# One piece of weights moved behind four pairs in every twelve-step chunk of a hybrid encoder layer

## The chip, the core and the metric

The kernel runs on one core of one Trainium2 chip. The metric is device time in microseconds (us), the median of repeated executions. The engines are named as in the profile: PE does matrix products (PEld loads its stationary operand), DVE works elementwise on tensors, ACT applies functions and copies, POOL is not used here beyond the start, SP issues the transfers (DMAs). Every engine takes its own instructions in order; one that must wait holds up all behind it on the same engine.

## What is computed

An input of 256 tokens by 4096 features is normalised, multiplied by an input projection 4096 x 13312, cut into the operands of a gated short convolution and of a windowed attention with 16 heads, multiplied by an output projection 4096 x 4096, added to the stream and normalised again. All in float32.

```python
h = layer_norm(x, emb_ln_g, emb_ln_b)
p = h @ w_in                       # 256 x 13312
y_conv = c_b * centred_short_conv(c_c * c_h, conv_w) * silu(c_z)
y_attn = banded_window_attention(a_q, a_k, a_v, sink) * silu(a_z)
y = concatenate([y_conv, y_attn]) @ w_out
out = layer_norm(DN_ALPHA * h + y, ln_g, ln_b)
```

## The kernel before

**Products in two parts.** PE gets float32 accuracy from a cheaper type by splitting each operand into a high part (a copy rounded by ACT, tile `whi`, line 226) and the rest (a subtraction on DVE, tile `wlo`, line 230). Three products are kept: high by high, low input by high weights, high input by low weights. Within a step PE first runs all products with `whi` and then those with `wlo`.

**Chunks.** The 13312 columns of the input projection are 26 chunks of 512 columns, numbered 0 to 25: K, V, then for each of four head groups the gate z and the queries q (chunks 2 to 9), then for each of four channel groups four convolution operands (10 to 25). The order of work inside a chunk is a string in `ORDERS`, written by hand:

- `s` is a **piece**: 4 blocks of 128 rows of weights, 1 MB, 48 matmuls of 256 columns (`mm`, line 275).
- `S` is a **pair**: 2 blocks of 128 rows, 512 KB, multiplied by a scheme after Strassen with seven products instead of eight, that is 21 matmuls (`mm_pair`, lines 300 to 303). It needs sums of weight blocks (DVE, `sums`, lines 192 to 194, made for two neighbouring pairs at once when they are "coupled") and sums of blocks of x (`x_sums`, made once and used by all later chunks).

A chunk of twelve steps (chunks 3 to 25) has four pieces and eight pairs. Positions count from 0 to 11 in a chunk; S4 means the pair at position 4, s5 the piece at position 5.

**What a step issues.** The loop at lines 835 to 859 goes over all steps j and writes, in this order: the products of step j; ACT's high part for step j+3; whatever `later` holds for step j; the end of a chunk at its position 3 of the following chunk (`chunk_end`, `whole`, line 717); `loads(j)`; the weight sums of step j+4; DVE's low part for step j+3. There are three `whi` and three `wlo` buffers, so the high part of step j+3 waits until PE has finished the `whi` products of step j, and the low part until PE has finished step j.

**Loads.** `loads` hands weights to four slots of `wall` and, for pieces, to `w6` as well (from chunk 13 on also `w7` and `w8`). Coupled pairs have to lie in `wall`. The next load goes out at step j when the last user of its buffer is step j+2 or earlier, and it waits for that user's low part. All these loads go through SP in order.

**Attention between the steps.** The work of a head group is cut into tasks with fixed distances t from the first step of the chunk after its queries (`SPREAD`, lines 661 to 663; t = 0 is position 0 of that chunk). The last two heads end in the chunk that follows 24 steps later: with t = 24 the turned probabilities of the third head (`p_tr`), with t = 27 their low part on DVE (`p_lo`, line 641, tile `kp`), with t = 28 the product with V on PE (`pv`, lines 648 and 650) and the turned probabilities of the fourth head, t = 29 `out_z` on DVE (line 654), t = 30 `p_lo` and t = 31 `pv` of the fourth head, which are positions 3, 4, 5, 6 and 7 of chunks 6, 8, 10 and 12. I call these four chunks the **tail chunks**. A `pv` waits on PE for its `p_lo` on DVE, and all later products wait behind it.

Of the kernel before, what the change touches and what calls it, by code (L numbers as in the profile page):

```python
# [34 lines left out]
NPC = KT // PK  # L35
# [7 lines left out]
NP = 8  # L43
NP1 = 4
PAIRS = [0, 0, NP1] + [NP] * (len(IN_ORDER) - 3)
ORDERS = {0: "s" * 8, NP1: "sssSSsSsSs", NP: "sSSsSSSSsSSs"}
OUT = 100
OP = 4
OUT_ORDERS = ["s" * 8] * 2 + ["sSsSsSsSss"] * 5 + ["", ""]
# [6 lines left out]
def units(ci):  # L56


    q, p, us = -(-2 * PAIRS[ci] // PK), 0, []
    for u in ORDERS[PAIRS[ci]]:  # L60
        if u == "s":
# [40 lines left out]
def encoder_kernel(ctx: ExitStack, tc: tile.TileContext, x, emb_g, emb_b, wi, ws, conv_w, sink, wo, ln_g, ln_b, out):  # L102
# [397 lines left out]
    def build_tab():  # L500
        ti = pa.tile([P, 2, S], F32, name="ti", tag="s")
        nc.gpsimd.iota(ti, pattern=[[-P, 2], [1, S]], base=0, channel_multiplier=-1,
                       allow_small_or_imprecise_dtypes=True)
        tf = pa.tile([P, 2, S], F32, name="tf", tag="p", bufs=2)
        nc.vector.tensor_scalar(tf, ti, -1.0, None, op0=ALU.mult)
        nc.vector.tensor_tensor(tf, tf, ti, op=ALU.max)
        nc.vector.tensor_scalar(ti, tf, float(WINDOW), NEG, op0=ALU.is_gt, op1=ALU.mult)
        nc.vector.tensor_tensor(tab, ti, tf, op=ALU.subtract)
# [162 lines left out]
    def x_sums(p, t):  # L671

        x = xT[:, 2 * p:2 * p + 2, :]
        xf = t[:, 0:2 * S].rearrange("p (k t) -> p k t", k=2)
        nc.vector.tensor_tensor(xf, x[:, :, 0:S].bitcast(F32), x[:, :, S:2 * S].bitcast(F32), op=ALU.add)
        a11, a12, a21, a22 = (xf[:, k, i * HT:(i + 1) * HT] for i in range(2) for k in range(2))
        s = t[:, 2 * S:4 * S].rearrange("p (k t) -> p k t", k=4)
        for k, o0, o1, op in ((0, a21, a22, ALU.subtract), (3, s[:, 0, :], a11, ALU.subtract),
                              (1, a11, a21, ALU.subtract), (2, a12, s[:, 3, :], ALU.add)):
            nc.vector.tensor_tensor(s[:, k, :], o0, o1, op=op)  # L680
        if SC[p].shape[2] == 4:
            return halves(SC[p][:, 0, :, :], SC[p][:, 1, :, :], s)
        halves(SC[p][:, 0, :, :], SC[p][:, 1, :, :], s[:, 0:3, :])
        halves(x[:, 0, HT:2 * HT], x[:, 0, 3 * HT:4 * HT], s[:, 3, :])
# [97 lines left out]
        for hi, lo, y in y_parts(q):  # L782
            nc.vector.tensor_tensor(lo, y, hi.bitcast(F32), op=ALU.subtract)

    X_SUMS = [NPC + 2 + k for k in range(NP1)] + [2 * NPC + k for k in (1, 4, 6, 8)]
    build_tab()
    later = {}

    def at(j, fn, *a):
        later.setdefault(j, []).append((fn, a))  # L790
# [36 lines left out]
    nxt = n_pro + 7  # L827
    last0 = N_IN - len(ORDERS[PAIRS[-1]])
    for t, f, q in ((3, y_load, 0), (5, y_hi, 0), (6, y_lo, 0), (6, y_load, 1), (7, y_hi, 1), (8, y_lo, 1), (8, y_load, 2),
# [5 lines left out]
    for j in range(n_pro, N_IN):  # L835
# [9 lines left out]
        if kind == "pair" and q == PAIRS[ci] - 1:  # L845
            pair_copy(ci)
            at(j + 1, pair_sums, ci)
        if j in X_SUMS:
            x_sums(X_SUMS.index(j), pa.tile([P, 4 * S], F32, name="xs", tag="zT", bufs=2))
        if steps[j + 1][1] != ci or j == N_IN - 1:  # L850
# [318 lines left out]
```

## Time and profile before

| | |
|---|---|
| median of three runs | 1501.05 us (1500.09 to 1501.15) |
| the profiled execution: its own time | 1500.92 us |
| its span, first to last instruction | 1499.2 us |
| granted PE clock | 0.999 |
| ACT busy | 803.3 us (54%) |
| SP's queue q1, share of the 16 DMA engines | 57.3% |

The profile lists instructions with their start and duration in us. Matmuls overlap: a row shows one as 0.28 us, but in an unbroken run the next starts 0.11 us later. So a stretch without a wait is read from starts to starts, and a wait on PE is a start that comes later than the one before it by more than 0.11 us. Rows of two DVE instructions in a row overlap by some 0.07 us as well, and are read in the same way. "[0.58 <-DVE kp L641]" behind a row is the idle time before it, and what ended it.

### The profile page before, as it was taken

How to read it: one execution, taken by the hardware profiler on the slowest of the kernel's cores; microseconds unless marked ns; L12 is line 12 of the kernel's file. 1: busy time of each engine (PE TensorE's matmuls, PEld its weight loads, DVE VectorE, ACT ScalarE, POOL GpSimd, SP SyncE). 2: the span in 40 equal slices, each digit the busy share in tenths (PEclk: the TensorE clock that was granted, in tenths of full speed). 3: DMA queues.
4: the chain of work that ended last, by engine and by line, in shares of the span. 5: the costliest groups of instructions: out<-in, count | busy, mean ns of one | idle time of the engine just before them, and what ended most of it. 6: DMA issues, size and time to landing. Idle time of an engine off the chain costs nothing.

```text
span 1499.2 us, 29810 instructions
## 1 busy us (share of the span) xinstructions
PE 1482.4 (99%) x12878; PEld 1465.4 (98%) x12878; DVE 1338.4 (89%) x1384; ACT 803.3 (54%) x687; POOL 1.3 (0%) x7
## 2 busy tenths in 40 slices
PE   7999999999999999999999999999999999999998
PEld 4999999999999999999999999999999999999997
DVE  7768999898999999999999999999998688888876
ACT  5544656766666665655555555555555444444431
POOL 0000000000000000000000000000000000000000
PEclk9999999999999999999999999999999999999999
DMA  8545465555554556646545655556558656756663
GB/s 318 217 183 196 164 217 189 192 197 208 180 204 176 190 201 209 230 177 224 200 182 219 231 198 197 225 204 241 191 207 313 233 201 220 290 215 230 219 237 113
DMA packets 71365, 316.17 MB, mean 211 GB/s; under 512 B 8545, under 2 KB 12609, under 8 KB 50113
## 3 DMA queue, kind: packets, MB, share of 16 engines
q1 hardware_dynamic: 70224, 312.43, 57.3%
q8 instruction: 101, 1.65, 0.4%
q10 hardware_dynamic: 1008, 1.84, 0.3%
q14 instruction: 32, 0.25, 0.0%
HBM read 305.23 MB, written 8.91 MB: 210 GB/s over the span
## 4 chain that ended last, share of the span: by engine, by line
PE 93%; DVE 3%; ACT 1%; issue 1%; DMA 1%; SPq 0%; ACTq 0%; DVEq 0%
PE acc L275 39%; PE acc L957 20%; PE pacc L301 6%; PE pacc L300 6%; PE pacc L303 6%; PE acc L301 4%; PE acc L300 4%; PE acc L303 4%; DVE wlo L230 1%; PE att L518 1%; ACT whi L226 1%; DVE st L354 0%; PE acc L404 0%; DMA wall<-in_ws 0%; DVE wall L192 0%
## 5 line engine op out<-in xcount | busy, mean ns | idle before, releaser
L226 ACT ACTIVATE whi<-wall 128x1792 fp32r<-128x1792 f32 (+1 forms) x284 | 501.7, 1772 | 464.6 <-DVE wall L194 149.7
L230 DVE TENSOR_TENSOR wlo<-wall,whi 128x1792 fp32r<-128x1792 f32 (+1 forms) x284 | 593.4, 2096 | 75.9 <-ACT whi L226 64.3
L275 PE MATMUL acc<-whi,xT 128*128 128x256 f32 x3584 | 427.6, 276 | 0.0
L275 PEld LDWEIGHTS acc<-whi,xT 128*128 128x128 f32 x3584 | 415.8, 188 | 0.0
L275 PE MATMUL acc<-wlo,xT 128*128 128x256 f32 x1792 | 221.3, 275 | 0.0
L275 PEld LDWEIGHTS acc<-wlo,xT 128*128 128x128 f32 x1792 | 211.4, 188 | 0.0
L226 ACT ACTIVATE whi<-w 128x2048 fp32r<-128x2048 f32 x73 | 140.7, 1927 | 114.6 <-PE acc L275 72.5
L957 PE MATMUL acc<-whi,xT 128*128 128x256 f32 x1696 | 201.8, 275 | 0.0
L957 PEld LDWEIGHTS acc<-whi,xT 128*128 128x128 f32 x1696 | 196.6, 188 | 0.4 <-issue 0.4
L230 DVE TENSOR_TENSOR wlo<-w,whi 128x2048 fp32r<-128x2048 f32 x73 | 166.8, 2286 | 10.8 <-ACT whi L226 10.6
L192 DVE TENSOR_TENSOR wall<-wall 128x1024 f32<-128x1024 f32 x93 | 113.3, 1218 | 11.0 <-DMA wall<-in_ws 8.7
L300 PE MATMUL acc<-whi,xT 128*128 128x256 f32 x416 | 114.7, 276 | 0.0
L301 PE MATMUL acc<-whi,xT 128*128 128x256 f32 x416 | 114.6, 276 | 0.0
L300 PE MATMUL pacc<-whi,xT 128*128 128x256 f32 x396 | 111.0, 280 | 0.0
L303 PE MATMUL pacc<-wlo,xT 128*128 128x256 f32 x396 | 109.2, 276 | 0.6 <-DVE wlo L230 0.4
L301 PE MATMUL pacc<-whi,xT 128*128 128x256 f32 x396 | 109.1, 276 | 0.0
L957 PE MATMUL acc<-wlo,xT 128*128 128x256 f32 x848 | 105.3, 275 | 0.0
L303 PE MATMUL acc<-wlo,xT 128*128 128x256 f32 x416 | 104.4, 275 | 0.0
L300 PE MATMUL pacc<-whi,SC 128*128 128x256 f32 x376 | 103.6, 275 | 0.0
L301 PE MATMUL pacc<-whi,SC 128*128 128x256 f32 x376 | 103.6, 275 | 0.0
L957 PEld LDWEIGHTS acc<-wlo,xT 128*128 128x128 f32 x848 | 100.4, 188 | 0.0
L303 PE MATMUL pacc<-wlo,SC 128*128 128x256 f32 x376 | 94.5, 276 | 0.0
(224 smaller groups left out, 1930.1 us busy)
## 6 DMA issues: line engine op xcount, KB each, us to landing
wall<-in_ws SPq DMA_DIRECT2D x202, 512.0 KB
w<-in_wi SPq DMA_DIRECT2D x73, 1024.0 KB
wall<-in_wo SPq DMA_DIRECT2D x43, 1024.0 KB
wall<-in_wi SPq DMA_DIRECT2D x39, 1024.0 KB
R<-in_wo SPq DMA_DIRECT2D x10, 1024.0 KB
x<-in_x SPq DMA_DIRECT2D x7, 512.0 KB
yl<-yd SPq DMA_DIRECT2D x7, 512.0 KB
xc<-in_x SPq DMA_DIRECT2D x14, 256.0 KB
```

The source lines that it names most:

```text
L192: nc.vector.tensor_tensor(t[:, :, 4:6, :], t[:, :, 1:3, :], t[:, :, 0:1, :].to_broadcast([P, 2, 2, HW]), op=ALU.add)
L226: nc.scalar.activation(part(j, wh[j]), part(j, raw[j]), AF.Copy)
L230: nc.vector.tensor_tensor(part(j, wl[j]), part(j, raw[j]), part(j, wh[j]).bitcast(F32), op=ALU.subtract)
L275: nc.tensor.matmul(acc[ci, i][:, c:c + HW], x, w[:, k * W + c:k * W + c + HW], start=(first and w is hi and k + off + c == 0), stop=(last ...
L300: nc.tensor.matmul(o, ah, hi[:, w, :], start=(opens and p == 0), stop=False)
L301: nc.tensor.matmul(o, al, hi[:, w, :], start=False, stop=False)
L303: nc.tensor.matmul(o, ah, lo[:, w, :], start=False, stop=(closes and last))
L518: nc.tensor.transpose(ps[:, c, i * P:(i + 1) * P], t[:, i, (2 * b + c) * P:(2 * b + c + 1) * P], ident)
L957: nc.tensor.matmul(acc[ci, i][:, c:c + HW], y, m[:, k * w + c:k * w + c + HW], start=(first and off + c == 0), stop=(last and c + HW == w))
```

## The change

In every twelve-step chunk the piece at position 3 changes places with the pairs at positions 4 and 5. The twelve steps were piece, two pairs, piece, four pairs, piece, two pairs, piece; they are now piece, four pairs, piece, two pairs, piece, two pairs, piece. Nothing is added or taken away. The tasks in `later` keep their positions, so at positions 3 and 4 other products stand around them. The sum of x for the eighth pair (`x_sums`, index 7) moves from step 24 (position 8 of chunk 2) to step 31 (position 5 of chunk 3).

```diff
-ORDERS = {0: "s" * 8, NP1: "sssSSsSsSs", NP: "sSSsSSSSsSSs"}
+ORDERS = {0: "s" * 8, NP1: "sssSSsSsSs", NP: "sSSSSsSSsSSs"}
...
-    X_SUMS = [NPC + 2 + k for k in range(NP1)] + [2 * NPC + k for k in (1, 4, 6, 8)]
+    X_SUMS = [NPC + 2 + k for k in range(NP1)] + [2 * NPC + k for k in (1, 4, 6, 15)]
```

**A tail chunk on DVE.** These are DVE's rows at the front of chunk 6 (the other tail chunks read alike), from the last sum of the chunk before (`q`, line 712) to the first `p_lo` (`kp`, line 641). `wlo` is a low part, from `wall` or `w`, 1792 columns for a pair and 2048 for a piece; `wall<-wall` are the three rows of one sum of weights. Before:

```order
L712 TENSOR_TENSOR q<-pacc,q 128x256
L230 TENSOR_TENSOR wlo_3202<-wall,whi 128x1792
L192 TENSOR_TENSOR wall<-wall 128x2x512
L193 TENSOR_TENSOR wall<-wall 128x2x256
L194 TENSOR_TENSOR wall<-wall 128x2x256
L230 TENSOR_TENSOR wlo_3266<-w_3042,whi 128x2048
L230 TENSOR_TENSOR wlo_3301<-wall,whi 128x1792
L192 TENSOR_TENSOR wall<-wall 128x2x512
L193 TENSOR_TENSOR wall<-wall 128x2x256
L194 TENSOR_TENSOR wall<-wall 128x2x256
L230 TENSOR_TENSOR wlo_3330<-wall,whi 128x1792
L641 TENSOR_TENSOR kp<-att,kp 128x512
```

And now:

```order
L712 TENSOR_TENSOR q<-pacc,q 128x256
L192 TENSOR_TENSOR wall<-wall 128x2x512
L193 TENSOR_TENSOR wall<-wall 128x2x256
L194 TENSOR_TENSOR wall<-wall 128x2x256
L230 TENSOR_TENSOR wlo_3206<-wall,whi 128x1792
L230 TENSOR_TENSOR wlo_3267<-wall,whi 128x1792
L230 TENSOR_TENSOR wlo_3301<-wall,whi 128x1792
L192 TENSOR_TENSOR wall<-wall 128x2x512
L193 TENSOR_TENSOR wall<-wall 128x2x256
L194 TENSOR_TENSOR wall<-wall 128x2x256
L230 TENSOR_TENSOR wlo_3330<-w_3130,whi 128x2048
L641 TENSOR_TENSOR kp<-att,kp 128x512
```

The first sum of weights (for S3 and S4) now stands ahead of the low part of S2, and the low part of the piece has moved from three rows after that sum to the place just ahead of `p_lo`. The number of rows ahead of `p_lo` is the same.

**The same place on PE.** PE's rows around the first `pv` of chunk 6 (lines 648 and 650; line 634 turns the fourth head's probabilities), from the end of S4 on. Before:

```order
L303 MATMUL pacc<-wlo_3301,SC 128x256
L648 MATMUL att<-kp,v 128x256 x4
L650 MATMUL att<-kp,v 128x256 x2
L634 MATMUL att<-ident,p 128x128 x4
L300 MATMUL pacc<-whi,xT 128x256
L301 MATMUL pacc<-whi,xT 128x256
```

And now:

```order
L303 MATMUL pacc<-wlo_3301,SC 128x256
L648 MATMUL att<-kp,v 128x256 x4
L650 MATMUL att<-kp,v 128x256 x2
L634 MATMUL att<-ident,p 128x128 x4
L275 MATMUL acc<-whi,xT 128x256 x32
L275 MATMUL acc<-wlo_3330,xT 128x256 x16
```

The `pv` stands behind S4 in both. The piece (line 275, 48 matmuls), which stood ahead of S4, now stands behind the `pv`.

**A tail chunk on SP.** The loads of the back of chunk 6, from the load of the piece s8 to the store of a head (`yd`); `in_ws` are pairs and `in_wi` pieces. Before:

```order
L172 DMA w_3299<-in_wi 128x2048
L172 DMA wall<-in_ws 128x1024 x2
L172 DMA wall<-in_wi 128x2048
L655 DMA yd_72<-zT 128x256
L172 DMA wall<-in_wi 128x2048
```

And now:

```order
L172 DMA wall<-in_wi 128x2048
L172 DMA wall<-in_ws 128x1024 x2
L172 DMA w_3397<-in_wi 128x2048
L655 DMA yd_72<-zT 128x256
L172 DMA wall<-in_wi 128x2048
```

The rows are in the same order, but the pieces have changed buffers: s8 now lies in `wall` and s11 in `w6`. By the rule of `loads`, S10 therefore goes out at position 4 instead of 3, and s11, whose buffer is free by then, right behind it in the same step. In the same way the load of S4 now goes out one step ahead of the step that sums it, with s5 right behind it. Before, that held for S2 alone (with s3 right behind it) and the others had two steps; now S4 and S10 have one, and S2 and S7 two.

## The prediction

> **What bounds the kernel now.** I read the page first, then the list of waits, then the order of time around the waits that PE has.
>
> ```profile
> span 1499.2 us, 29810 instructions
> PE 1482.4 (99%) x12878; PEld 1465.4 (98%) x12878; DVE 1338.4 (89%) x1384; ACT 803.3 (54%) x687; POOL 1.3 (0%) x7
> ```
>
> PE is the bound and DVE comes close behind. The change takes no work from either, so it can only take away or add waits of PE. The list of waits, PE's own, has three that lie where the order changes:
>
> ```profile
> PE att L648 <- DVE kp L641: 1.6, 3, 0.6
> PE att L518 <- DVE m L601: 0.7, 2, 0.6
> PE pacc L303 <- DVE wlo L230: 0.4, 1, 0.4
> ```
>
> The columns are us in total, times, longest. The list counts from the modelled end of a matmul, which is 0.28 us after its start, while the next one would start after 0.11; so each wait is some 0.17 us more. That makes 2.1 us for three `pv` (L648), 1.0 us for two transposes of z (L518). The third kind is low parts that come late, in chunk 3:
>
> ```profile
> 173.10 0.28 PE L301 MATMUL pacc<-whi,SC 128*128 128x256 f32 x1
> 173.51 0.39 PE L303 MATMUL pacc<-wlo,xT 128*128 128x256 f32 x1
> ...
> 175.92 0.28 PE L301 MATMUL pacc<-whi,SC 128*128 128x256 f32 x1
> 176.64 0.39 PE L303 MATMUL pacc<-wlo,xT 128*128 128x256 f32 x1 [0.45 <-DVE wlo L230]
> ```
>
> These starts are 0.41 and 0.72 us apart instead of 0.11: 0.3 and 0.6, 0.9 us in all. All that the change could win is thus about 4 us.
>
> **The clock of PE in a tail chunk** (chunk 8, from the start of S1):
>
> ```profile
> 383.55 0.36 PE L300 MATMUL pacc<-whi,xT 128*128 128x256 f32 x1
> ...
> 386.41 0.36 PE L300 MATMUL pacc<-whi,xT 128*128 128x256 f32 x1
> ...
> 388.92 3.79 PE L275 MATMUL acc<-whi,xT 128*128 128x256 f32 x32
> ...
> 394.36 0.28 PE L300 MATMUL pacc<-whi,xT 128*128 128x256 f32 x1
> ...
> 396.74 0.61 PE L648 MATMUL att<-kp,v 128*128 128x256 f32 x4
> ...
> 397.78 0.36 PE L300 MATMUL pacc<-whi,xT 128*128 128x256 f32 x1
> ...
> 405.42 0.28 PE L303 MATMUL pacc<-wlo,SC 128*128 128x256 f32 x1
> 406.27 0.70 PE L648 MATMUL att<-kp,v 128*128 128x256 f32 x4 [0.58 <-DVE kp L641]
> ```
>
> S1 with a transpose behind it takes 2.86 us, the piece s3 5.44 (388.92 to 394.36), a pair 2.38 (S4, to 396.74), the first `pv` with the transposes behind it 1.04. S5, S6, a transpose and S7 take 7.75 (397.78 to 405.53). Then the second `pv` waits 0.74 us for its `p_lo`.
>
> **The clock of DVE there**, with ACT's high part that releases a low part:
>
> ```profile
> 388.20 2.02 DVE L230 TENSOR_TENSOR wlo<-wall,whi 128x1792 fp32r<-128x1792 f32 x1
> 390.14 1.22 DVE L192 TENSOR_TENSOR wall<-wall 128x1024 f32<-128x1024 f32 x1
> ...
> 392.73 2.02 DVE L230 TENSOR_TENSOR wlo<-wall,whi 128x1792 fp32r<-128x1792 f32 x1
> 394.66 0.68 DVE L641 TENSOR_TENSOR kp<-att,kp 128x512 fp32r<-128x512 f32 x1
> 395.26 1.28 DVE L717 TENSOR_TENSOR q<-acc,q 128x512 f32<-128x512 f32 x2
> 396.46 3.95 DVE L230 TENSOR_TENSOR wlo<-wall,whi 128x1792 fp32r<-128x1792 f32 x2
> 400.33 0.41 DVE L654 TENSOR_TENSOR zT<-att,zT 128x256 f32<-128x256 f32 x1
> 400.66 1.21 DVE L192 TENSOR_TENSOR wall<-wall 128x1024 f32<-128x1024 f32 x1
> ...
> 403.24 2.28 DVE L230 TENSOR_TENSOR wlo<-w,whi 128x2048 fp32r<-128x2048 f32 x1
> 405.45 0.68 DVE L641 TENSOR_TENSOR kp<-att,kp 128x512 fp32r<-128x512 f32 x1
> ```
>
> ```profile
> 396.20 1.71 ACT L226 ACTIVATE whi<-wall 128x1792 fp32r<-128x1792 f32 x1 [1.51 <-PE pacc L301]
> ```
>
> From start to start: low part of a pair 1.94 us, a coupled sum 2.59, `p_lo` 0.60 (0.68 to its end), `whole` 1.20, `out_z` 0.33, low part of a piece 2.21. The high part starts 1.84 us after the pair whose buffer it takes (394.36 to 396.20) and takes 1.71, so a low part that waits for nothing else starts 3.55 us after the start of the pair three steps ahead. From the end of a `p_lo` (406.13) to its `pv` (406.27) pass 0.14.
>
> **The first pv: new wait, the largest term.** Count from the start of S1. Now three pairs and no piece stand between S1 and the `pv`: PE is there at 2.86 + 3 x 2.38 = 10.0 us. DVE cannot begin the low part of S4 before 3.55; then come that part (1.94), the sum for S6 and S7 (2.59), the low part of s5 (2.21) and `p_lo` (0.68): 10.97, and with 0.14 the `pv` starts at 11.1. **PE waits 1.1 us** in chunks 6, 8 and 10. Before, PE had 3.06 us more (a piece in place of a pair) and DVE was done 1.4 us ahead (395.34 to 396.74). In chunk 12 the head that gave S1 its transpose is over, PE is there at 9.5, and the wait is 1.6. Sum: 3 x 1.1 + 1.6 = **+4.9**.
>
> This needs DVE to be free at 3.55. It is, by this row and the next ones:
>
> ```profile
> 366.87 0.38 SPq L172 DMA_DIRECT2D wall<-in_ws  x1
> 367.30 0.44 SPq L172 DMA_DIRECT2D w<-in_wi  x1
> ...
> 371.46 1.22 DVE L192 TENSOR_TENSOR wall<-wall 128x1024 f32<-128x1024 f32 x1 [2.22 <-issue]
> ...
> 381.48 2.02 DVE L230 TENSOR_TENSOR wlo<-wall,whi 128x1792 fp32r<-128x1792 f32 x1
> ```
>
> At 371.46 DVE had stood 2.2 us for the load of S2, issued at 366.87 with a piece right behind it. That load now goes out a step earlier and this wait goes. Before, DVE reached the low part of S2 at 381.48, 2.07 us ahead of S1 (383.55). Without the 2.2 us lost, and with 0.7 us less for PE at the transpose of z, it is there 3.6 us ahead; with a sum and two low parts (2.59 + 2 x 1.94 = 6.5) ahead of the low part of S4, it is free at 2.9, 0.6 us early. Only if the load of S4 is over 0.6 us late does it add its lateness.
>
> **The second pv.** Count on: `p_lo` gives way at 10.9 us, `whole` ends at 12.1, the low part of S6 at 14.0. Its end sends the load of S10, and s11 follows at once. A couple behind such a load began to sum 4.6 us after the issue (366.87 to 371.46); I take 4.4, as nothing else is in flight: 18.4. DVE has only 2.3 us of other work in between and stands. Then sum, low part of s8, `p_lo`, 0.14: 24.0. PE leaves the first `pv` at 11.1 + 1.04, does s5 (5.44), S6 and S7 with the transpose (7.75 - 2.38 = 5.37): 22.95. The wait is 1.1 us instead of 0.74 in chunks 6, 8 and 10; about the same in chunk 12, where s11 comes a step later. Sum: **+1.2**. A load alone is faster:
>
> ```profile
> 376.37 0.33 SPq L172 DMA_DIRECT2D wall<-in_ws  x1
> ...
> 376.00:379.50 3.50, 2.92 (x26) 2.73 (x25) 3.46 (x8) 2.14 (x8) 0.00 (x0) 1.00 0.40 150
> ```
>
> 150 GB/s over 3.5 us is the whole 512 KB, so it was in 3.1 us after its issue. Bounds of this term: with 3.1 us DVE is done at 22.7, before PE, and the old waits go (-2.1); with 6.2, twice that, the wait is 2.9 (+6.5).
>
> The Trainium skill speaks to this point: its page "DMA: Bandwidth & Descriptors", section "Queues, rings and completion order", says that each DMA engine consumes the descriptors of one ring in ring order. By that rule s11, issued later on the same queue, would not slow S10, and the load would take the 3.1 us; the trace does not bear it out, as the one with a piece behind it took up to 4.6.
>
> **What goes.** The two transposes of z waited for DVE at the end of chunks 5 and 7, behind the DVE waits for the load of S2; with those gone they are in time: **-1.0**. In chunk 3 the low parts were late behind the eighth sum of x:
>
> ```profile
> 151.96 0.68 DVE L675 TENSOR_TENSOR xs<-xT 128x512 f32<-128x512 f32 x1
> ...
> 154.97 2.02 DVE L230 TENSOR_TENSOR wlo<-wall,whi 128x1792 fp32r<-128x1792 f32 x1
> ```
>
> It holds DVE for 3.0 us, just ahead of chunk 3. Now it stands behind the run of pairs, ahead of the sum for S9 and S10 and the low part of s8: from 3.55, DVE needs 1.94 + 2.59 + 2.21 + 1.20 + 2 x 1.94 + 3.0 + 2.59 + 2.21 = 19.6, done at 23.2. PE needs that part two thirds into s8, at 4 x 2.38 + 5.44 + 2 x 2.38 + 3.63 = 23.35. Just in time; I take 0.2 late: **-0.7** net.
>
> **What stays.** In the convolution chunks the same count holds with a product (like L192's 1.22) in place of the 3.0: done at 21.4, 1.9 us early, and three buffers more carry the loads. In the query chunks `p_lo`, `whole` and a `s_add` fall on the same places, and DVE stands for S10; the low part of s8 is done near 23.3, PE needs it near 25, since a `pv`, scores and transposes stand between. Both: 0. Were that cover gone, each of about 20 chunks would pay what it is late. The output stage and the tail are untouched.
>
> **The sum.** 4.9 + 1.2 - 1.0 - 0.7 = +4.4. The profiled execution took 1500.92 us by its own time (0.13 below the median 1501.05): **1505.3 us**, 0.3% slower. About 0.2%, 3.0 us, is what a measurement of this kernel can tell from no change.
>
> **The rivals.**
> - *Loads side by side cost nothing* (a queue that serves them one after another). The first `pv` still waits, the second ones no longer: 4.9 - 2.1 - 1.0 - 0.7 = +1.1, 1502.0 us. For it speaks that loads alone do take 3.1; against it 371.46.
> - *Faster: DVE is ahead at the first pv.* If the block from the low part of S4 to the end of `p_lo` (7.42 us) began 1.1 us earlier or was that much shorter, neither `pv` would wait and all old waits would go: -2.1 - 1.0 - 0.7 = -3.8, 1497.1 us. It decides at 10.0 us from S1. Against it: ACT's high part cannot start before the products of S1 that hold its buffer, and each part of the block has its row.
> - *Slower still: the load of S4 is late in each tail chunk*, with s5 beside it and as little lead as S2 had. The 2.2 us of the row at 371.46, less 0.6 of room, four times: +6.4, 1511.7 us. For it speaks that row; against it that a pair's low part and four sums of the last chunk stand on DVE between issue and need.
>
> **How the numbers follow.** Forecast 0.55: its own range is 1503 to 1508, and about a fifth of it lies within the bound. Side by side for nothing 0.24. Faster 0.09. Late loads 0.12. Slower by over 0.2%: 0.45 + 0.12 = 0.57. Within: 0.10 + 0.24 = 0.34. Faster: 0.09. The range from 1500.5 to 1509.8 leaves out the faster case and the upper half of the late loads, some 15%.
>
> **What would show it.** Right: `pv` waits on `kp` seven or eight times instead of three, at positions 4 and 7 of chunks 6, 8, 10 and 12, each near 1 us; L518 no longer waits for `m`; DVE waits for `in_ws` at the sums of S9 and S10; no wait of L303 on `wlo` before 180 us. Wrong: no `pv` wait behind S4 (then DVE was ahead), or waits of L275 and L303 on `wlo` in many chunks (then four pairs in a row starve PE, which I hold for covered).

## The result, and the profile after

| | before | after |
|---|---|---|
| median | 1500.95 us (1500.09 to 1501.71, 20 runs) | 1502.93 us (1502.06 to 1504.68, 20 runs) |
| profiled execution, its own time | 1500.92 | 1502.40 |
| its span | 1499.2 | 1500.4 |

The ratio is 1.0015 with an interval of 1.0009 to 1.0022: slower by 0.15%, more than chance would give, but less than the 0.2% that the prediction set as its bound. The forecast was 1505.3, its range 1500.5 to 1509.8.

The page of the changed kernel begins as before; no engine got work:

```profile
span 1500.4 us, 29793 instructions
...
PE 1482.7 (99%) x12878; PEld 1465.6 (98%) x12878; DVE 1339.8 (89%) x1384; ACT 800.4 (53%) x687; POOL 1.3 (0%) x7
```

PE's own waits, from the list of waits (us in total, times, longest):

```profile
PE att L650 <- DVE kp L641: 2.3, 5, 0.9
PE att L648 <- DVE kp L641: 1.5, 3, 0.6
...
PE acc L275 <- DVE wlo L230: 0.2, 1, 0.2
```

The three `pv` waits of the list before are eight (a fourth before, 0.34 us in chunk 12, was too short for that list); the waits of L518 and of L303 are gone. The one of L275 is the low part of s8 in chunk 3, 0.46 us. How the chunks changed, from the first product of a chunk to that of the next (us):

| chunk | 3 | 4 | 5 | 6 | 7 | 8 | 9 | 10 | 11 | 12 | 13 to 24 |
|---|---|---|---|---|---|---|---|---|---|---|---|
| before | 42.99 | 43.15 | 45.25 | 46.96 | 45.66 | 46.91 | 44.93 | 46.96 | 44.51 | 44.38 | 40.80 to 41.79 |
| after | 42.30 | 43.15 | 44.87 | 47.46 | 44.98 | 47.62 | 44.85 | 47.35 | 44.49 | 45.88 | the same |

The four tail chunks lost 3.1 us; chunks 3, 5 and 7 won 1.75. Chunks 9 and 11 won another 0.1. The balance of these chunks is +1.3, that of the profiled executions +1.5, that of the medians +2.0.

**Where the first `pv` waits.** PE in chunk 8 (start, duration, what ended the idle time):

```profile
392.61 0.28 PE L303 MATMUL pacc<-wlo,SC 128*128 128x256 f32 x1
392.72 0.61 PE L648 MATMUL att<-kp,v 128*128 128x256 f32 x4
393.71 0.51 PE L650 MATMUL att<-kp,v 128*128 128x256 f32 x2 [0.37 <-DVE kp L641]
...
398.17 1.98 PE L275 MATMUL acc<-wlo,xT 128*128 128x256 f32 x16
...
405.12 0.28 PE L303 MATMUL pacc<-wlo,SC 128*128 128x256 f32 x1
406.04 0.70 PE L648 MATMUL att<-kp,v 128*128 128x256 f32 x4 [0.64 <-DVE kp L641]
```

At the first `pv` (392.72) the four matmuls of L648 start at once and only L650 waits; from 392.72 to 393.71 are 0.99 us where four matmuls take 0.45. At the second (405.12 to 406.04) L648 itself waits, 0.81 us beyond the 0.11 of a matmul.

**DVE there**, with SP's issue of S10's load and of the piece behind it:

```profile
379.66 1.22 DVE L192 TENSOR_TENSOR wall<-wall 128x1024 f32<-128x1024 f32 x1
...
388.18 1.22 DVE L192 TENSOR_TENSOR wall<-wall 128x1024 f32<-128x1024 f32 x1
...
390.77 2.28 DVE L230 TENSOR_TENSOR wlo<-w,whi 128x2048 fp32r<-128x2048 f32 x1
392.97 0.68 DVE L641 TENSOR_TENSOR kp<-att,kp 128x512 fp32r<-128x512 f32 x1
...
400.41 1.23 DVE L192 TENSOR_TENSOR wall<-wall 128x1024 f32<-128x1024 f32 x1 [1.36 <-DMA wall<-in_ws]
...
405.21 0.68 DVE L641 TENSOR_TENSOR kp<-att,kp 128x512 fp32r<-128x512 f32 x1
```

```profile
396.81 0.33 SPq L172 DMA_DIRECT2D wall<-in_ws  x1
397.18 1.03 SPq L172 DMA_DIRECT2D w<-in_wi  x1
```

At 379.66 the sum of S3 and S4 and at 388.18 that of S6 and S7 start without a wait, and the block from there to the end of the first `p_lo` (393.65) has no gap: it is what the prediction counted (from the start of S1 at 382.60 to 393.65 are 11.05 us, where it had 10.97). At 400.41 DVE has stood 1.36 us for S10's load, but it began 3.6 us after the issue (396.81), where the prediction took 4.4.

### The profile page after: what moved, and what is told of

Read it like the earlier page. It is cut to its first block, busy times and chain, and to the rows that moved or that the text cites. A ratio compares the mean times of both kernels' runs of the same rounds, so it can differ in the third digit from the quotient of the medians.

```text
span 1500.4 us, 29793 instructions
## 1 busy us (share of the span) xinstructions
PE 1482.7 (99%) x12878; PEld 1465.6 (98%) x12878; DVE 1339.8 (89%) x1384; ACT 800.4 (53%) x687; POOL 1.3 (0%) x7
## 4 chain that ended last, share of the span: by engine, by line
PE 95%; DVE 3%; ACT 1%; DMA 0%; issue 0%; SPq 0%; DVEq 0%; ACTq 0%
PE acc L275 40%; PE acc L957 20%; PE pacc L301 6%; PE pacc L300 6%; PE pacc L303 6%; PE acc L301 4%; PE acc L300 4%; PE acc L303 4%; DVE wlo L230 1%; PE att L518 1%; DVE st L354 0%; PE att L634 0%; PE acc L404 0%; DMA x<-in_x 0%; PE att L648 0%
## 5 line engine op out<-in xcount | busy, mean ns | idle before, releaser
L275 PE MATMUL acc<-whi,xT 128*128 128x256 f32 x3584 | 428.0, 277 | 0.0
L275 PEld LDWEIGHTS acc<-whi,xT 128*128 128x128 f32 x3584 | 415.9, 188 | 0.0
L275 PE MATMUL acc<-wlo,xT 128*128 128x256 f32 x1792 | 221.5, 276 | 0.2 <-DVE wlo L230 0.2
L275 PEld LDWEIGHTS acc<-wlo,xT 128*128 128x128 f32 x1792 | 211.5, 188 | 0.4 <-DVE wlo L230 0.4
L303 PE MATMUL pacc<-wlo,xT 128*128 128x256 f32 x396 | 109.1, 276 | 0.0
L303 PE MATMUL acc<-wlo,xT 128*128 128x256 f32 x416 | 104.4, 276 | 0.0
L303 PE MATMUL pacc<-wlo,SC 128*128 128x256 f32 x376 | 94.5, 276 | 0.0
```

The lines of the kernel that those rows point to most:

```text
L275: nc.tensor.matmul(acc[ci, i][:, c:c + HW], x, w[:, k * W + c:k * W + c + HW], start=(first and w is hi and k + off + c == 0), stop=(last ...
L303: nc.tensor.matmul(o, ah, lo[:, w, :], start=False, stop=(closes and last))
```

## The experiments

Each kernel was timed beside the kernel before on the same chip: 1500.93 us for plo2, plo3, plo23 and after_again, 1500.90 for order_only, sum_only, before_plo23 and hold, 1500.43 for store_last, before_hold and best. Waits in the text are from start to start, less the 0.11 us of a matmul, and with the up to 0.1 us by which the matmuls behind a wait come late as well.

### p_lo a step earlier

If the first `pv` waits because `p_lo` ends a chain on DVE that is too long for three pairs, `p_lo` one step earlier, ahead of the sum and the low part of s5, has to end it. *plo2* moves that of the third head, *plo3* that of the fourth, *plo23* both:

```diff
-... head(2, 13, 17, 18, 19, 20, 24, 27, 28, 29) + head(
-        3, 21, 22, 22, 23, 23, 28, 30, 31, 32)
+... head(2, 13, 17, 18, 19, 20, 24, 26, 28, 29) + head(
+        3, 21, 22, 22, 23, 23, 28, 29, 31, 32)
```

> The changed kernel with one number changed: the low part of the third head (p_lo) stands at position 2 of the tail chunks instead of 3, so ahead of a sum of weights and of the low part of s5. Theory (the first pv waits for a p_lo that stands too far back on DVE): the four waits of L650 behind S4 (3 x 0.64 + 1.14 = 3.06 us in the profile) go. But the second pv is set by DVE's queue, in which nothing is shorter, and PE comes there earlier by just that: the second wait grows from about 0.7 to about 1.3 us in chunks 6, 8 and 10 and by up to 1.1 in chunk 12, and the time stays within 1 us of the changed kernel (1502.9). Rival (the pv waits are hidden slack and the time was lost to loads that come a step later): neither the waits nor the time move. Rival (the two waits are independent): 1499.9 us.

1502.52 us (1501.95 to 1503.29), ratio 1.0010 [1.0001, 1.0019]. The list of waits of plo2:

```profile
PE att L648 <- DVE kp L641: 3.7, 3, 1.5
PE att L650 <- DVE kp L641: 1.4, 1, 1.4
```

The first waits are gone, and the second ones have grown from between 0.6 and 0.9 us to between 1.3 and 1.7. The late work stays late on DVE; PE only meets it three steps further on.

> The changed kernel with one number changed: the low part of the fourth head stands at position 5 of the tail chunks instead of 6, so ahead of the sum for S9 and S10, for whose load DVE stands idle, and of the low part of s8. Theory: the second pv waits (0.69, 0.88, 0.63, 0.64 us in the profile) go, nothing else moves: 1502.9 - 2.8 = 1500.1 us, and the first waits at L650 stay at 0.64 and 1.14. Rival (time lost to late loads of S10, which then show up as low parts of s8 that come late): the wait moves to L275 in s8 and the time stays at 1502.9.

1499.60 us (1499.18 to 1501.82), ratio 0.9992 [0.9983, 1.0001]. The second waits are gone, the four first ones stay as they were (from the list of waits of plo3, which has one more of 0.5 us at L592, in chunk 7):

```profile
PE att L650 <- DVE kp L641: 2.0, 4, 0.9
```

So the two kinds of wait are two claims on DVE, and the second does not need the first.

> The changed kernel with both p_lo one position earlier. Theory: all eight pv waits go, 3.06 + 2.84 = 5.9 us: 1497.0 us, faster than both kernels; PE's list of waits has no kp left. Rival (loads are the limit): the waits come back as late low parts (L275 or L303 on wlo) in the tail chunks, and less than 3 us is won.

1496.87 us (1496.17 to 1497.63), ratio 0.9973 [0.9963, 0.9984]. No wait on `kp` is left, and the tail chunks take 46.12, 46.12, 46.12 and 44.00 us, 0.8 and 0.4 less than before the change.

> The changed kernel itself, a second profile beside the others on the same chip. Theory: eight pv waits again, each within 0.2 us of the first profile, 1502.9 us. Rival (the 2 us are chance of one set of executions): the ratio's interval to the kernel before takes in 1.

The changed kernel once more: 1503.09 us (1501.99 to 1503.90), ratio 1.0014 [1.0005, 1.0023]. The same eight waits, but the second one of chunk 8 took 1.6 us instead of 0.9, since S10's load came 0.8 us later there. Its time hangs on the landing of four such loads, which would fit its wider spread.

### The two halves of the change

*order_only* has the new order with the eighth sum of x at its old place (the diff, against the changed kernel), *sum_only* the old order with the sum moved:

```diff
-    X_SUMS = [NPC + 2 + k for k in range(NP1)] + [2 * NPC + k for k in (1, 4, 6, 15)]
+    X_SUMS = [NPC + 2 + k for k in range(NP1)] + [2 * NPC + k for k in (1, 4, 6, 8)]
```

> The new order with the eighth sum of x left at step 24 (position 8 of chunk 2). Theory: the sum (3.0 us of DVE) then stands ahead of a run of four pairs; the low parts of the first pairs of chunk 3 come later than before, where PE has one piece fewer to spend, so PE waits at L303 on wlo in chunk 3 for 1.5 to 2 us: chunk 3 takes 43.8 to 44.3 us instead of 42.3, and the time is about 1504.7 us. The eight pv waits in the tail chunks stay. Rival: the place of the sum does not matter, chunk 3 stays at 42.3 and the time is that of the change, 1502.9.

1506.74 us (1505.05 to 1508.44, 5 runs), ratio 1.0038 [1.0025, 1.0052]. The direction was expected, the place and the size were not: at L303, where the wait was expected, PE loses 0.3 us, but in s8 2.0, and chunk 3 takes 45.95 us, 3.65 more than with the sum moved. DVE, and then PE:

```profile
180.18 1.23 DVE L192 TENSOR_TENSOR wall<-wall 128x1024 f32<-128x1024 f32 x1 [2.88 <-DMA wall<-in_ws]
```

```profile
181.73 1.52 PE L275 MATMUL acc<-whi,xT 128*128 128x256 f32 x12
185.11 3.30 PE L275 MATMUL acc<-wlo,xT 128*128 128x256 f32 x16 [1.86 <-DVE wlo L230]
```

With the sum early, the load of S9 and S10, which waits for a low part, goes out late (at 175.4 instead of 173.1, right behind that low part in both), and DVE stands 2.88 us for it. In the changed kernel it does the sum in that place, from its first row to the sum of the weights behind it:

```profile
174.93 0.69 DVE L675 TENSOR_TENSOR xs<-xT 128x512 f32<-128x512 f32 x1
...
178.11 1.22 DVE L192 TENSOR_TENSOR wall<-wall 128x1024 f32<-128x1024 f32 x1
```

Of these 3.2 us PE feels only 0.46, the wait for the low part of s8. In order_only that low part comes 2.0 us late. On top of that its 16 matmuls take 3.30 us instead of 1.98 (the row at 398.17 in the changed kernel's chunk 8): the clock has fallen. The view by stretches (width, busy time and count of PE, PEld, DVE, ACT, POOL, then granted clock, DMA share, GB/s):

```profile
183.00:185.00 2.00, 0.26 (x3) 0.06 (x1) 2.00 (x2) 1.98 (x2) 0.00 (x0) 1.00 0.10 37
185.00:187.00 2.00, 1.89 (x11) 1.89 (x12) 2.00 (x3) 2.00 (x2) 0.00 (x0) 0.68 0.44 135
187.00:189.00 2.00, 2.00 (x12) 2.00 (x11) 2.00 (x2) 1.11 (x1) 0.00 (x0) 0.50 0.80 262
189.00:191.00 2.00, 2.00 (x19) 2.00 (x18) 2.00 (x1) 0.69 (x2) 0.00 (x0) 0.96 0.83 272
```

By these shares of the clock PE runs at half speed for 3.4 us, from about 0.6 us after the wait to a little after 189; a matmul takes 0.21 us instead of 0.11. That costs 1.7 us, about what the expectation lacked.

> The old order with the eighth sum of x moved to step 31. Theory: the waits at S5 and S6 of chunk 3 (0.9 us together) go, but the sum then stands ahead of the low part of a piece close by and this comes late by about as much: chunk 3 takes 42.3 to 43.5 us, the tail chunks are as before (three pv waits), time 1500.3 to 1501.3. Rival: the whole gain of chunk 3 (0.7 us) comes from the sum and nothing from the order: chunk 3 at 42.0 to 42.3 and 1500.0 to 1500.3.

1500.81 us (1500.36 to 1501.90), ratio 1.0001 [0.9992, 1.0009]. Chunk 3 takes 43.31: the waits at S5 and S6 are gone, and the low part of s8 is late by as much (profile of sum_only):

```profile
184.02 2.14 PE L275 MATMUL acc<-wlo,xT 128*128 128x256 f32 x16 [1.21 <-DVE wlo L230]
```

The gain of chunk 3 needs both halves: each alone is worth nothing or costs 3 us.

### What the order is worth without its pv waits

*before_plo23* is the old order with both `p_lo` a step earlier (the diff of plo23).

> The old order with both p_lo tasks one step earlier (t 26 and 29). Theory: the second pv waits of the old order (2.1 by the list, 2.7 from start to start) go; the waits of the transposes of z (1.0) and of chunk 3 (0.9), which the new order took away, stay: 1498.0 to 1498.6, that is some 1.5 us above the new order with the same two edits (1496.9). Rival: what the new order won is only in its tasks, and both orders with early p_lo come to the same time, 1496.9.

1498.18 us (1497.60 to 1499.63), ratio 0.9983 [0.9975, 0.9992]. No wait on `kp` is left, those of the transposes of z and of chunk 3 are. It is 2.7 below its kernel before; plo23 was 4.1 below its own. With `p_lo` out of the way the new order is thus 1.3 us faster than the old one by the medians. The two intervals overlap, but the profiles show where the difference comes from: the new order takes 0.7, 0.5 and 1.0 us less in chunks 3, 7 and 9.

### Which neighbour slows a load

The prediction took 4.4 us for S10's load, for the piece issued right behind it. *hold* is the changed kernel with that piece held back by a step in chunks 4 to 12 (`sent` is the last load that this call of `loads` issued):

```diff
-            if u > j + (2 if j >= n_pro else 3):
+            if u > j + (2 if j >= n_pro else 3) or 3 < steps[nxt][1] < 13 and not is_pair(nxt) and sent == nxt - 1 and is_pair(sent):
```

> The change, with one edit to the loads: in chunks 4 to 12 a piece's load is held back by one step where it would follow a pair's load in the same step, so the load of S10 in the tail chunks travels without s11 behind it. Theory of the prediction (a load right behind slows the one ahead): DVE's wait for S10's load in the tail chunks falls from 1.1-1.4 us to 0.7 or less, the second pv waits fall by as much, by 0.5 each and 2 us in all: about 1501. Rival (the transfers are served in the order of their issue): DVE's wait and the second pv waits stay as they are, 1502.9. The first pv waits (3.1 in all) stay under both.

1502.84 us (1501.58 to 1503.84), ratio 1.0014 [1.0005, 1.0023], as the changed kernel. SP and DVE in chunk 6, first of the changed kernel and then of hold:

```profile
304.38 0.33 SPq L172 DMA_DIRECT2D wall<-in_ws  x1
304.76 0.42 SPq L172 DMA_DIRECT2D w<-in_wi  x1
...
307.78 1.23 DVE L192 TENSOR_TENSOR wall<-wall 128x1024 f32<-128x1024 f32 x1 [1.16 <-DMA wall<-in_ws]
```

```profile
304.25 0.33 SPq L172 DMA_DIRECT2D wall<-in_ws  x1
306.52 0.33 SPq L655 DMA_DIRECT2D yd<-zT  x1
306.94 0.38 SPq L172 DMA_DIRECT2D w<-in_wi  x1
...
307.62 1.23 DVE L192 TENSOR_TENSOR wall<-wall 128x1024 f32<-128x1024 f32 x1 [1.13 <-DMA wall<-in_ws]
```

The piece now goes out 2.7 us behind the load instead of 0.4, and the sum starts 3.4 us after the issue in both. In chunk 10 it is 3.3 and 3.4, in chunk 12, where no piece followed in either kernel, 3.4 in both. In chunk 8 it is 3.6 with the piece behind and 4.3 without. A transfer behind a load costs it nothing that could be seen here; what may have made chunk 8 late comes below.

What was it then at 366.87, the row the 4.6 us were read from? There the row ahead, which the prediction did not show, is a store (kernel before):

```profile
366.45 0.33 SPq L655 DMA_DIRECT2D yd<-zT  x1
366.87 0.38 SPq L172 DMA_DIRECT2D wall<-in_ws  x1
367.30 0.44 SPq L172 DMA_DIRECT2D w<-in_wi  x1
```

*store_last* is the old order with the stores of line 655 issued behind the loads of their step; *before_hold* is the old order with the edit of hold:

```diff
-        nc.sync.dma_start(out=yd[h // GROUP][:, h % GROUP, :], in_=y)
+        stores.append((yd[h // GROUP][:, h % GROUP, :], y))
...
         loads(j)
+        while stores:
+            o, i = stores.pop(0)
+            nc.sync.dma_start(out=o, in_=i)
```

> The old order with one edit: the store of a finished head (yd, 128 KB) is issued behind the weight loads of its step instead of ahead of them. In the old order such a store stood directly ahead of the load of S2 at the ends of chunks 5 and 7, the load whose 4.1 us from its issue to landing the prediction took for the cost of the piece behind it. Theory now: a transfer ahead is what slows a load. The load of S2 then lands about 3 us after its issue and also goes out up to 0.4 us earlier, DVE's wait of 2.2 us at its sum falls to about 0.8, the z transposes at the ends of chunks 5 and 7 no longer wait for DVE, chunks 5 and 7 take 44.9 instead of 45.3 and 45.7, time 1499.6 to 1500.2. The pv waits may change by a few tenths. Rival (the prediction's reading, the piece behind it slows it): load 4.1 us, wait about 2, chunks 5 and 7 as before, 1500.9.

1498.83 us (1498.29 to 1499.28), ratio 0.9989 [0.9980, 0.9998]. SP and DVE at the same place:

```profile
365.58 0.33 SPq L172 DMA_DIRECT2D wall<-in_ws  x1
365.96 0.43 SPq L172 DMA_DIRECT2D w<-in_wi  x1
366.44 0.42 SPq L861 DMA_DIRECT2D yd<-zT  x1
...
368.88 1.23 DVE L192 TENSOR_TENSOR wall<-wall 128x1024 f32<-128x1024 f32 x1 [0.17 <-DMA wall<-in_ws]
```

The sum starts 3.3 us after the issue instead of 4.6, with the same piece right behind the load. At the same place of chunks 5 and 9 it is 3.3 in store_last too, and 4.2 and 3.9 in the kernel before. Chunks 5 and 7 take 44.87 us, and the second `pv` waits of chunks 6, 8 and 10 shrink from 0.8 to between 0.3 and 0.4 us, since DVE kept the time it won until then (in chunk 8 the second `p_lo` ends 22.1 us after the start of S1 instead of 22.6). The expectation gave these waits a few tenths at most and no price; with them the gain is 1.6 us, where 0.7 to 1.3 were expected.

The 4.6 of chunk 7 is not the store's alone. The DMA view of the kernel before from 366.87 to 371.46 has this line:

```profile
q8 instruction: 1, 0.02, 1.2%
```

The columns are packets, MB and share of the 16 DMA engines: one packet of 16 KB of another queue, which starts 1.3 us behind the load; at the same loads of chunks 5 and 9 there is none. So a store ahead goes with 0.6 to 0.9 us, and the rest of the 4.6 is probably that packet's. It also goes with the other late loads: of the 72 loads of S10 in chunks 4 to 12 in the eight profiles with the new order, where nothing is issued in the 7.9 us ahead of the load, ten took over 4 us to the sum (4.2 to 5.0; chunk 8 of hold and of after_again are among them), and all ten have such a packet from 0.2 us before to 2.9 us after their issue. The 56 without one took 3.1 to 3.8, six others with one 3.3 to 3.6. No run took these packets away.

> The old order with the other neighbour of that load moved: in chunks 4 to 12 a piece's load is held back by one step where it would follow a pair's load in the same step, so the load of S2 travels with the store ahead of it but no piece right behind. Theory now: nothing gained, the load of S2 at the ends of chunks 5 and 7 lands 4 us after its issue, DVE waits about 2.2 us, the z transposes wait as before, 1500.9 (to 1501.5, since the piece itself comes later). Rival (the prediction's reading): the load takes 3.1 us, the waits of the z transposes go, chunks 5 and 7 at 44.9, 1499.9.

1500.71 us (1500.33 to 1501.02), ratio 1.0001 [0.9992, 1.0010]. The number is the expected one, but the run tells nothing: SP stood before the store, and when it came free, load and piece went out 0.44 us apart as before, whatever step they were written in. That the piece costs nothing rests on hold.

### A version that beats both

*best* is plo23 with the eighth sum of x at step 32 (16 in place of 15 in `X_SUMS`), behind the low part of s8. "Both" are the kernels before and after; its interval and that of plo23 overlap.

> The version that the runs point to: the new order, both p_lo tasks one step earlier, and the eighth sum of x one step later still (step 32, behind the low part of s8 instead of ahead of it). Expected: no wait on kp, and the wait of 0.46 at s8 of chunk 3 goes as well, so 0.4 to 0.5 below the kernel with the early p_lo alone (1496.9): 1496.4. Rival: the sum then delays the low parts or the products of S9 and S10 behind it in chunk 3 by as much: 1496.9 or more.

1495.83 us (1495.66 to 1496.16), ratio 0.9968 [0.9956, 0.9980]. Chunk 3 takes 41.79 us, as the convolution chunks of its kind. Between the input stage and the output stage one wait of PE is left, a product of the scores in chunk 7, where the load of S10 was one of the ten late ones (5.0 us):

```profile
PE att L592 <- DVE zT L654: 0.3, 1, 0.3
```

## Why the prediction was off in size

The mechanism was right: the change handed DVE's lost time to the `pv`. The signs that were named came as well: eight `pv` waits at positions 4 and 7 of the tail chunks, none of L518 for `m`, DVE standing for `in_ws` at the sums of S9 and S10, none of L303 in chunk 3. Only "each near 1 us" was too much. Two terms of the sum were mis-sized; all in us:

| term | predicted | measured |
|---|---|---|
| first `pv`, four chunks | +4.9 | +3.1 (0.64 three times, 1.14) |
| second `pv` | +1.2 | +0.1 (0.69, 0.88, 0.63, 0.64; before 0.77, 0.83, 0.77, 0.34) |
| transposes of z (chunks 5 and 7) | -1.0 | -1.1 |
| chunk 3 | -0.7 | -0.7 |
| query and convolution chunks | 0 | 0 in each, within 0.1 |

- **First `pv`.** The step that failed is "From the end of a `p_lo` (406.13) to its `pv` (406.27) pass 0.14": it put the whole wait ahead of L648. DVE came when it was counted to, but L648 multiplies the high part only; its four matmuls, 0.45 us, run while DVE works. 4 x 0.45 = 1.8 is the whole difference. The row it was read from is a second `pv`, where L648 does wait. I explain that by the tile: `att` has two buffers, `q_tr` (line 518) takes one just ahead (402.37 us in chunk 8), and the one left is what `p_lo` still reads. In chunk 12, which has no `q_tr` there, L650 waits, not L648. The semaphores in the trace bear this out: the first L648 of the second `pv` waits for DVE's semaphore in chunks 6, 8 and 10, and not in chunk 12, nor at any first `pv`. No run gave `att` a third buffer.
- **Second `pv`.** The step that failed is "A couple behind such a load began to sum 4.6 us after the issue (366.87 to 371.46); I take 4.4". It named the wrong neighbour. S10's sum began 3.3 to 3.6 us after the issue. In chunk 8 that was 17.8 us after the start of S1, where 18.4 were counted, since the load also went out 0.2 us later than counted; PE came 0.3 us earlier than counted. 1.1 - 0.6 + 0.3 = 0.8, and 0.81 was measured from start to start (0.88 with the late matmuls behind).
- **The rule that the prediction set aside.** The Trainium skill, page "DMA: Bandwidth & Descriptors", section "Queues, rings and completion order", has each DMA engine take a ring's descriptors in order; the prediction said that the trace does not bear it out. hold and store_last agree with it: 3.4 us with a piece behind as without it, and with the store moved behind the load 3.3 instead of 3.9 to 4.6.
- **The rivals.** "Loads side by side cost nothing" had the loads right and came nearest by its number, 1502.0; but it let the second waits go, and they stayed, because 3.4 us from the issue to the sum still leave DVE standing. "The load of S4 is late" fell: the sum of S3 and S4 starts without a wait (379.66 in chunk 8, and likewise in the other tail chunks). "DVE is ahead at the first `pv`" fell in the changed kernel, and plo23 shows what it would have given: 1496.9 against 1497.1.
- **Chance.** Slower by over 0.2% had 0.57. A gap of 2.0 us came out, inside the bound, which had 0.34; 1502.9 lies just under the 1503 to 1508 that the forecast gave itself, and nearer to the rival's number. The two terms were both too high, so they did not cancel.

## What to carry to other kernels

Of a wait that moves to another place, read which instruction of the group needs the late operand: those ahead of it run on, and a row from another place may wait for a buffer instead. Where a load looks slow, look at what stands ahead of it on its queue, and at packets of other queues, before blaming what follows, read the same load in several chunks, and put small stores behind the loads that are needed soon. When a change only moves slack about, look for the small task at the end of the late chain: here two `p_lo` written one step earlier turned +2.0 us into -4.1.

## What the runs showed of the hardware

A wait of PE of 2.0 us (order_only) was followed by 3.4 us at a granted clock of 0.5, which cost another 1.7 us; waits of 1.6 us in after_again and plo2 and of 1.4 in sum_only were not. The Trainium skill, page "TensorE: Matmul & The Clock Gate", section "What's actually happening", names an idle window of about 3.4 us for this; here 2.0 us sufficed, in the one profile that shows it, so a wait near 2 us cost nearly twice its length.
